# Gate operand sums made one stage earlier, in the space of x, with another order of the gate weights and other accumulator banks

## The chip, the cores and the metric

The kernel runs on one core of a Trainium2 chip. The metric is the device time of one execution in microseconds, lower is better; the median of three runs is 2232.85 us (2231.98 to 2233.49).

## The reference, cut to what matters

One decoder layer on 256 tokens of width 2048, in fp32:

```python
x = layer_norm(ALPHA * x + 0.5 * swiglu(x, ffn1_w_in, ffn1_w_out), ...)
z = x @ mix_w_in                     # conv B | C | h | hgrn q | f | i | g | gate_conv | gate_hgrn
y_conv = short_conv_mixer(b_gate, c_gate, h_conv, conv_w)
y_hgrn = hgrn2_mixer(q_raw, f_raw, i_in, g_raw, lower_bounds, hg_norm_w)
merged = (sigmoid(gate_conv) * (y_conv @ branch_w_conv)      # gate_*: 2048 columns each of z
          + sigmoid(gate_hgrn) * (y_hgrn @ branch_w_hgrn))   # branch weights: 1024 x 2048
x = layer_norm(ALPHA * x + merged @ mix_w_out, ...)
x = layer_norm(ALPHA * x + 0.5 * swiglu(x, ffn2_w_in, ffn2_w_out), ...)
x = layer_norm(ALPHA * x + sigmoid(x @ ple_w_gate) * (p @ ple_w_proj), ...)
```

## The kernel before, in words

All weights (some 430 MB) stream from memory once, in pieces of 512 KB: 256 rows by 512 columns, as a tile of 128 partitions by 1024 numbers. SP issues each load into one of four raw slots (NRAW, tile `raw`, L969). An fp32 product is made of three fast ones: ScalarE casts the raw weight to its high half `wh` (L1029), VectorE subtracts to get the low half `wl` (L1040), and TensorE multiplies high by high, low by high and high by low (L1096, L1097, L1098). The operand x1 (x after the first layer norm, transposed) is kept in such halves too, `xh` and `xl`, made in L288 and L289. The split in L1040 is the last reader of a raw slot, so it lets the next load of that ring start. `wh` and `wl` live in pairs of slots: NMAIN = 6 pairs for all, and EXTRA more in some stages, for the elements that are marked for them (two of eight, in plain units only); a pair comes free when TensorE has used it.

The plan is a list of units: plain ones (`Unit`) and `Quad`s. A Quad computes two column blocks of 512 with seven products for eight, after Strassen's manner, for half of the depth; its weight elements are named in a string (ORDER): `11`, `22`, `21` are loaded pieces, `t1` to `t4` sums of loaded pieces (made by VectorE in L1008 in raw slots of rings of their own, HIGH, where a piece waits until its last sum), each with the step 0 or 1 behind the dot; `a0` to `a3` and `u0` to `u3` are the plain pieces of the other half of the depth, for the first and the second column block. The products of t1, 22, t3 and t2 need sums of x1's four parts, s1 to s4 (tiles `sh`, `sl`).

The stages follow each other: lead1, ffn1, tail1, hgrn, merge, lead2, ffn2, tail2, ple. In the hgrn stage the conv and hgrn parts of z are computed, with the chunked recurrence, and the two mixers' outputs `ya` and `yb` are transposed into halves `gh` and `gl`; its last tiles are b (L768), transposed by TensorE (L278), and `z` (L774). The merge stage has for each of four column blocks c one Quad for the two gates, then two units of four elements each, called conv and hgrn here (`branch_w_conv`, `branch_w_hgrn`; in the texts c.0 to c.3 and h.0 to h.3). Each such element has six products for each of two token tiles t. Then come four units of mix_w_out.

`gate_sums` runs at the head of the merge stage: four additions give x1's parts in whole (L797), `four` (L312) the four combinations, and `halves` (L288, L289) casts and splits them. `settle` and `affine_rows` (L398, L399) apply the first layer norm's scale and shift to the plain x, column block by column block, in the hgrn stage; x itself (two tiles of 128 x 2048) is next read behind the merge stage, at the sum with mix_w_out's result (L876).

Accumulators are eight banks of PSUM; `ptile` gives out the bank whose last handing out is longest ago. `defer` puts small pieces of work some elements later. A scheduler sorts the instructions of each engine by a simulated timeline when the program is built, and each engine then runs its own in that order.

## Time and profile before

| | us |
|---|---|
| median of three runs | 2232.85 |
| the profiled execution | 2234.01 |
| its span, first to last instruction | 2232.3 |
| TensorE busy (98% of the span) | 2192.5 |
| VectorE busy (81%) | 1809.8 |
| ScalarE busy (53%) | 1173.6 |
| GpSimd busy | 10.1 |
| hgrn stage | 720 to 1062 |
| gate quads and branch units | 1062 to 1345 |

The profile is of one execution. Its page gives busy times and the chain of work that ended last; the trace behind it is asked by stretch, engine or line. Matmuls overlap, so a row's duration (0.39 us) is longer than the distance to the next row (0.23 us). Line numbers are those of the kernel before, except in the rows of the changed program below.

### The profile page before, as it was taken

How to read it: one execution, taken by the hardware profiler on the slowest of the kernel's cores; microseconds unless marked ns; L12 is line 12 of the kernel's file. 1: busy time of each engine (PE TensorE's matmuls, PEld its weight loads, DVE VectorE, ACT ScalarE, POOL GpSimd, SP SyncE). 2: the span in 40 equal slices, each digit the busy share in tenths (PEclk: the TensorE clock that was granted, in tenths of full speed). 3: DMA queues.
4: the chain of work that ended last, by engine and by line, in shares of the span. 5: the costliest groups of instructions: out<-in, count | busy, mean ns of one | idle time of the engine just before them, and what ended most of it. 6: DMA issues, size and time to landing. Idle time of an engine off the chain costs nothing.

```text
span 2232.3 us, 27072 instructions
## 1 busy us (share of the span) xinstructions
PE 2192.5 (98%) x10038; PEld 1823.3 (82%) x10038; DVE 1809.8 (81%) x2046; ACT 1173.6 (53%) x1393; POOL 10.1 (0%) x32
## 2 busy tenths in 40 slices
PE   9999999999999999999899999999999999999997
PEld 7988888888877888888687788798888888888886
...
GB/s 255 217 193 205 208 207 192 193 193 208 206 207 105 208 169 172 187 171 156 209 168 185 186 179 217 174 203 193 193 198 198 202 213 200 201 212 178 181 209 153
DMA packets 225848, 429.99 MB, mean 193 GB/s; under 512 B 14252, under 2 KB 22964, under 8 KB 225716
## 3 DMA queue, kind: packets, MB, share of 16 engines
...
q14 instruction: 54, 0.44, 0.1%
...
## 4 chain that ended last, share of the span: by engine, by line
PE 90%; DVE 4%; DMA 2%; ACT 2%; issue 1%; SPq 0%; DVEq 0%; ACTq 0%
PE bank L1097 29%; PE bank L1096 29%; PE bank L1098 29%; DVE wl L1040 2%; PE bank L278 2%; ACT wh L1029 1%; PE bank L634 1%; DVE raw L1008 1%; DMA raw<-in_branch_w_hgrn_dram 1%; DMA raw<-in_ffn_w_in_dram 0%; DMA raw<-in_ffn_w_out_dram 0%; DVE silu L460 0%; DVE x L435 0%; DMA raw<-in_mix_w_in_dram 0%; DMA x<-in_x_dram 0%
## 5 line engine op out<-in xcount | busy, mean ns | idle before, releaser
L1029 ACT CAST wh<-raw 128x1024 fp32r<-128x1024 f32 (+1 forms) x968 | 971.9, 1031 | 802.3 <-PE bank L1098 409.8
L1040 DVE TENSOR_TENSOR wl<-raw,wh 128x1024 fp32r<-128x1024 f32 (+1 forms) x968 | 1137.1, 1201 | 266.7 <-ACT wh L1029 249.4
L1098 PE MATMUL bank<-wh,xl 128*128 128x512 f32 (+1 forms) x1672 | 646.7, 388 | 1.4 <-DVE xl L289 1.4
L1097 PE MATMUL bank<-wl,xh 128*128 128x512 f32 (+1 forms) x1672 | 647.9, 388 | 0.1
L1096 PE MATMUL bank<-wh,xh 128*128 128x512 f32 (+1 forms) x1672 | 639.2, 389 | 2.6 <-ACT xh L288 1.6
L1096 PEld LDWEIGHTS bank<-wh,xh 128*128 128x128 f32 x1672 | 315.5, 189 | 63.5 <-ACT xh L288 2.3
L1098 PEld LDWEIGHTS bank<-wh,xl 128*128 128x128 f32 x1672 | 315.3, 189 | 62.3 <-DVE xl L289 2.3
L1097 PEld LDWEIGHTS bank<-wl,xh 128*128 128x128 f32 x1672 | 315.3, 189 | 59.8 <-DVE wl L1040 0.7
L1096 PE MATMUL bank<-wh,gh 128*128 128x512 f32 x896 | 348.4, 395 | 10.7 <-ACT wh L1029 7.5
L1097 PE MATMUL bank<-wl,gh 128*128 128x512 f32 x896 | 350.8, 393 | 2.6 <-DVE wl L1040 2.2
L1098 PE MATMUL bank<-wh,gl 128*128 128x512 f32 x896 | 349.8, 392 | 0.0
L1008 DVE TENSOR_TENSOR raw<-raw,raw 128x1024 f32<-128x1024 f32 x208 | 245.0, 1181 | 10.6 <-DMA raw<-in_ffn_w_in_dram 7.4
L1096 PEld LDWEIGHTS bank<-wh,gh 128*128 128x128 f32 x896 | 169.2, 189 | 48.4 <-ACT wh L1029 10.4
L1097 PE MATMUL bank<-wl,sh 128*128 128x512 f32 x528 | 206.9, 392 | 0.7 <-DVE wl L1040 0.7
L1098 PE MATMUL bank<-wh,sl 128*128 128x512 f32 x528 | 205.7, 390 | 0.0
L1096 PE MATMUL bank<-wh,sh 128*128 128x512 f32 x528 | 202.4, 390 | 2.5 <-ACT wh L1029 2.5
L1097 PEld LDWEIGHTS bank<-wl,gh 128*128 128x128 f32 x896 | 168.9, 189 | 39.4 <-DVE wl L1040 5.4
L1098 PEld LDWEIGHTS bank<-wh,gl 128*128 128x128 f32 x896 | 168.9, 188 | 34.7
L1096 PEld LDWEIGHTS bank<-wh,sh 128*128 128x128 f32 x528 | 99.1, 188 | 23.8 <-ACT wh L1029 3.2
L1097 PEld LDWEIGHTS bank<-wl,sh 128*128 128x128 f32 x528 | 99.2, 188 | 21.7 <-DVE wl L1040 1.5
L1098 PEld LDWEIGHTS bank<-wh,sl 128*128 128x128 f32 x528 | 99.2, 188 | 20.2
L288 ACT CAST gh<-bank 128x512 fp32r<-128x512 f32 (+2 forms) x54 | 30.6, 569 | 77.5 <-PE bank L278 77.0
...
## 6 DMA issues: line engine op xcount, KB each, us to landing
raw<-in_ffn_w_in_dram SPq DMA_DIRECT2D x288, 512.0 KB, 4.3
...
raw<-in_ffn_w_in_dram SPq DMA_DIRECT2D x64, 256.0 KB, 3.0
...
```

What stands on the lines that cost most here:

```text
L278: state["turned"] = nc.tensor.transpose(tp[:, i * P : (i + 1) * P], src[:, i * P : (i + 1) * P], ident).ins
L288: nc.scalar.copy(hf, src)
L634: nc.tensor.matmul(gp[:, (h * 2 + t) * 64 : (h * 2 + t + 1) * 64], kd[:, h, t * P : (t + 1) * P], qd[:, h, t, :], start=True, stop=True)
L1008: nc.vector.tensor_tensor(out=out, in0=a, in1=b, op=ALU.add)
L1029: nc.scalar.copy(h[:, :n, :w], raw[:, :n, :w])
L1040: state["split"] = nc.vector.tensor_tensor(out=l[:, :n, :w], in0=raw[:, :n, :w], in1=h[:, :n, :w].bitcast(F32), op=ALU.subtract).ins
L1096: nc.tensor.matmul(acc, sh, wh[:, a, :n], start=first, stop=False)
L1097: nc.tensor.matmul(acc, sh, wl[:, a, :n], start=False, stop=False)
L1098: nc.tensor.matmul(acc, sl, wh[:, a, :n], start=False, stop=last)
```

## The change

Five things change together.

1. The sums s1 to s4 are made in the hgrn stage, from the copy of the second v on (`epi_v`, j = 1, first token tile), and not at the head of merge. They use three temporary tiles, and their halves are written into the space of x's two tiles.
2. For this x is stored to device memory, by eight transfers of 256 KB issued from GpSimd, each behind the affine of its column block, and loaded again by eight transfers from GpSimd at the end of the last gate quad.
3. All four quads use one ORDER, "gate", which interleaves a1 to a3 with the other elements; "gate0" is gone.
4. In gate quads a bank counts as used at each write to it (`used`), not only when it is handed out.
5. EXTRA for merge is 2 in place of 0: two more weight pairs, for two of the eight elements of the plain units.

```diff
-EXTRA = {..., "hgrn": 0, "merge": 0, ...}
+EXTRA = {..., "hgrn": 0, "merge": 2, ...}
-        "gate": "a0 a1 11.0 11.1 u0 t1.0 a2 22.0 t3.0 u1 t2.0 21.0 a3 t4.0 u2 t1.1 22.1 t3.1 u3 t2.1 21.1 t4.1",
-        "gate0": "a0 a1 a2 a3 11.0 11.1 u0 t1.0 22.0 t3.0 u1 t2.0 21.0 t4.0 u2 t1.1 22.1 t3.1 u3 t2.1 21.1 t4.1",
+        "gate": "a0 11.0 a1 11.1 a2 t1.0 u0 22.0 t3.0 u1 t2.0 21.0 u2 t4.0 t1.1 u3 22.1 t3.1 a3 t2.1 21.1 t4.1",
+        self.by_end = form == "gate"
     def ptile(role, name):
-        n = min(role_of[role], key=lambda n: used_at[n])
+        bank = banks[min(role_of[role], key=lambda n: used_at[n])]
+        used(bank)
+        return bank
+
+    def used(bank):
+        n = next(n for n in banks if banks[n] is bank)
         used_at[n] = max(used_at.values()) + 1
-        return banks[n]
-    def halves(stat, t, g, src, nb, tag):
+    def halves(stat, t, g, src, nb, tag, into=None):
+    def store_x(c):
+        for t in range(NT):
+            stored[t, c] = dram.tile([P, CC], F32, tag=f"x{t}{c}", name="stored")
+            nc.gpsimd.dma_start(stored[t, c], xt[t][:, c * CC : (c + 1) * CC])
+
+    def load_stored():
+        xt[:] = [res.tile([P, D], F32, tag=f"x{t}", name=f"x{t}") for t in range(NT)]
+        for c in range(4):
+            for t in range(NT):
+                nc.gpsimd.dma_start(xt[t][:, c * CC : (c + 1) * CC], stored[t, c])
+
+    def gate_sums():
+        def both(o, a, b, op):
+            nc.vector.tensor_tensor(out=o, in0=a, in1=b, op=op)
+        def whole(o, t, g):
+            both(o, *(a.rearrange("p a b -> p (a b)").bitcast(F32) for a in x1.parts[t, g]), ALU.add)
+        def made(n, src):
+            i = int(n[1]) - 1
+            into = [w[:, 4 * i : 4 * i + 4, :] for w in room_of_x]
+            halves(x1, n, 0, src, 4, "s", into)
+        room_of_x = [res.tile([P, 16, P], F32R, tag=f"x{t}", name="s") for t in range(NT)]
+        a, b = (rtile([P, CC], tag=f"sum{i}", name="sum") for i in range(2))
+        d = st.tile([P, CC], F32, tag="h", name="sum", bufs=3)
...
+        def s1():
+            whole(a, 1, 0)
+            whole(b, 1, 1)
+            both(b, a, b, ALU.subtract)
+            made("s1", b)
...
+        for i, fn in enumerate((s1, s3, s2, s4)):
+            defer(1 + 4 * i, fn)
+            if not early and stat is x1:          # in affine_rows
+                store_x(c)
         def epi_v(t, acc):
+            if j == 1 and t == 0:
+                gate_sums()
             if c == 3:                            # in gate_units, the last piece of a quad's work
                 share_banks({"a": 4, "t": 4})
+                load_stored()
-        units.append(Quad(x1, wm, cols, CC, after, "gate" if c else "gate0"))
+        units.append(Quad(x1, wm, cols, CC, after, "gate"))
-    units.append(("merge", gate_sums))
+                if u.by_end:                      # in run_quad, at each element
+                    used(ps[bank])
```

In the rows of the changed program below the same work has other line numbers: the products are L1149 to L1151, the cast of a weight L1082, its split L1093, the sum of raw weights L1061, halves L296 and L297, b L834, z L840.

TensorE at the turn from the first gate quad to its branch units. `wh_8880` and `wh_8894` are the first two weights of the hgrn branch (h.0, h.1) before, `wh_8816` the first of the conv branch; `wh_8877`, `wh_8896` and `wh_8910` are h.0, h.1 and h.2 after. Before:

```order
L1096 MATMUL bank0_79<-wh_8880,gh_7132 128x512
L1097 MATMUL bank0_79<-wl_8881,gh_7132 128x512
L1098 MATMUL bank0_79<-wh_8880,gl_7133 128x512
L1096 MATMUL bank0_79<-wh_8894,gh_7132 128x512
L1096 MATMUL bank7_86<-wh_8816,gh_7174 128x512
L1097 MATMUL bank7_86<-wl_8817,gh_7174 128x512
L1098 MATMUL bank7_86<-wh_8816,gl_7175 128x512
L1096 MATMUL bank7_86<-wh_8816,gh_7174 128x512
L1097 MATMUL bank7_86<-wl_8817,gh_7174 128x512
```

After:

```order
L1149 MATMUL bank5_86<-wh_8877,gh_7062 128x512
L1150 MATMUL bank5_86<-wl_8878,gh_7062 128x512
L1151 MATMUL bank5_86<-wh_8877,gl_7063 128x512
L1149 MATMUL bank5_86<-wh_8896,gh_7062 128x512
L1150 MATMUL bank5_86<-wl_8897,gh_7062 128x512
L1151 MATMUL bank5_86<-wh_8896,gl_7063 128x512
L1149 MATMUL bank5_86<-wh_8896,gh_7062 128x512
L1150 MATMUL bank5_86<-wl_8897,gh_7062 128x512
L1151 MATMUL bank5_86<-wh_8896,gl_7063 128x512
L1149 MATMUL bank5_86<-wh_8910,gh_8409 128x512
L1150 MATMUL bank5_86<-wl_8911,gh_8409 128x512
```

Before, TensorE turns to conv behind one product of h.1, and comes back to h.1 at the end of conv's first token tile; after, it goes on through the hgrn branch.

ScalarE in the hgrn stage behind the last affine of x (`r` is the root of the hgrn norm, `b` the tile that the conv part makes). Before:

```order
L671 ACTIVATE junk,ss<-bank_79 128x128 x4
L1029 CAST wh<-raw 128x1024
L367 ACTIVATE r<-w 128x4
L768 COPY b<-bank_86 128x512
L1029 CAST wh<-raw 128x1024 x3
L288 CAST gh<-bank_85 128x512
```

After:

```order
L735 ACTIVATE junk,ss<-bank_81 128x128 x4
L1082 CAST wh<-raw 128x1024
L429 ACTIVATE r<-w 128x4
L296 CAST s<-sum 128x512
L834 COPY b<-bank_88 128x512
L1082 CAST wh<-raw 128x1024 x3
L296 CAST gh<-bank_87 128x512
```

The cast of s1 (`s<-sum`) has come between the root and the copy of b, ahead of three casts of weights.

VectorE at the start of the merge stage; `gl<-z` is the last operand of the hgrn stage. Before:

```order
L774 TENSOR_TENSOR z<-bank_85,cT 128x512
L797 TENSOR_TENSOR xT<-xh,xl 128x512 x4
L289 TENSOR_TENSOR gl<-z,gh 128x512
L312 TENSOR_TENSOR xT<-xT 128x512
L1040 TENSOR_TENSOR wl<-raw_8527,wh 128x1024
L312 TENSOR_TENSOR xT<-xT 128x512
L1040 TENSOR_TENSOR wl<-raw_8529,wh 128x1024
L1008 TENSOR_TENSOR raw_8527<-raw_8527,raw_8531 128x1024
L312 TENSOR_TENSOR xT<-xT 128x512
L1040 TENSOR_TENSOR wl<-raw,wh 128x1024
L289 TENSOR_TENSOR sl<-xT,sh 128x512
L1008 TENSOR_TENSOR raw_8531<-raw_8531,raw_8533 128x1024
```

After:

```order
L840 TENSOR_TENSOR z<-bank_87,cT 128x512
L297 TENSOR_TENSOR gl<-z,gh 128x512
L1093 TENSOR_TENSOR wl<-raw_8548,wh 128x1024
L1093 TENSOR_TENSOR wl<-raw,wh 128x1024
L1061 TENSOR_TENSOR raw_8548<-raw_8548,raw_8552 128x1024
L1093 TENSOR_TENSOR wl<-raw_8550,wh 128x1024
L1093 TENSOR_TENSOR wl<-raw,wh 128x1024
L1061 TENSOR_TENSOR raw_8552<-raw_8552,raw_8554 128x1024
L1093 TENSOR_TENSOR wl<-raw_8548,wh 128x1024
L1093 TENSOR_TENSOR wl<-raw,wh 128x1024
L1093 TENSOR_TENSOR wl<-raw_8554,wh 128x1024
L1061 TENSOR_TENSOR raw_8548<-raw_8548,raw_8554 128x1024
```

The sums, differences and low halves of x1's parts are gone from there, and splits of weights (the a elements among them) stand in their place.

## Rows read from the trace of the kernel before

**Rows 1.** The head of the page: the busy time of TensorE, and the shares of the chain that ended last by engine.

```profile
PE 2192.5 (98%) x10038; PEld 1823.3 (82%) x10038; DVE 1809.8 (81%) x2046; ACT 1173.6 (53%) x1393; POOL 10.1 (0%) x32
PE 90%; DVE 4%; DMA 2%; ACT 2%; issue 1%; SPq 0%; DVEq 0%; ACTq 0%
```

**Rows 2.** Busy time by stretch. Columns: the stretch, its length, then for TensorE, its weight loads, VectorE, ScalarE and GpSimd the busy time and in brackets the number of instructions; behind them the granted TensorE clock, the DMA share and GB/s. The hgrn stage ends at 1062; the merge stage begins there.

```profile
720.00:1062.00 342.00, 342.00 (x1708) 288.89 (x1707) 231.20 (x330) 149.45 (x193) 3.41 (x3) 1.00 0.57 179
1062.00:1072.00 10.00, 9.31 (x42) 7.32 (x40) 9.80 (x13) 5.58 (x7) 0.00 (x0) 1.00 0.48 164
1072.00:1080.00 8.00, 5.76 (x22) 3.79 (x21) 8.00 (x9) 5.43 (x8) 0.00 (x0) 1.00 0.29 84
1080.00:1345.00 265.00, 254.60 (x1116) 208.37 (x1117) 216.10 (x216) 141.09 (x151) 0.00 (x0) 0.98 0.59 188
```

**Rows 3.** What TensorE waited for from 1062 to 1345 us: total, number of waits, longest.

```profile
PE bank L1096 <- ACT wh L1029: 10.6, 7, 5.7
PE bank L1097 <- DVE wl L1040: 2.7, 4, 0.8
```

**Rows 4.** Timeline of TensorE at the turn from the first gate quad to its branch units and behind it: start, duration, engine, line, operation, tiles; in brackets the idle time ahead and what ended it. Left out behind 1111.39 are the ten products up to 1116.08, and behind that the rest of the branch units. The last row is the first product of the second quad.

```profile
1103.45 0.39 PE L1098 MATMUL bank<-wh,xl 128*128 128x512 f32 x1
1109.54 0.80 PE L1096 MATMUL bank<-wh,gh 128*128 128x512 f32 x1 [5.70 <-ACT wh L1029]
...
1111.39 0.63 PE L1098 MATMUL bank<-wh,gl 128*128 128x512 f32 x1
...
1116.08 0.39 PE L1096 MATMUL bank<-wh,gh 128*128 128x512 f32 x1
...
1134.90 0.39 PE L1096 MATMUL bank<-wh,xh 128*128 128x512 f32 x1
```

**Rows 5.** Timeline of TensorE at the same turn of column blocks 1 and 2, and the load ahead of the latter in the chain that ended last (start, duration, what).

```profile
1176.59 0.50 PE L1096 MATMUL bank<-wh,gh 128*128 128x512 f32 x1 [0.72 <-ACT wh L1029]
...
1241.51 0.50 PE L1096 MATMUL bank<-wh,gh 128*128 128x512 f32 x1 [1.05 <-ACT wh L1029]
...
1234.72 5.60 DMA raw<-in_branch_w_hgrn_dram
```

**Rows 6.** Timeline of VectorE at the start of the merge stage: the rows of the operand sums (L797 sums, L289 low halves; the differences, L312, have the size of one low half).

```profile
1062.80 2.49 DVE L797 TENSOR_TENSOR xT<-xh,xl 128x512 f32<-128x512 f32 x4
...
1072.15 0.69 DVE L289 TENSOR_TENSOR sl<-xT,sh 128x512 fp32r<-128x512 f32 x1
...
1080.17 1.90 DVE L289 TENSOR_TENSOR sl<-xT,sh 128x512 fp32r<-128x512 f32 x3
```

**Rows 7.** Timeline of TensorE, VectorE and ScalarE around z: the transposes of b, z, the cast of z, the first cast of a weight behind it; and, of the turn in rows 4, the cast whose product starts at 1109.54.

```profile
1061.56 0.60 PE L278 MATMUL bank<-ident,b 128*128 128x128 f32 x4
...
1062.20 0.69 DVE L774 TENSOR_TENSOR z<-bank,cT 128x512 f32<-128x512 f32 x1 [3.59 <-PE bank L278]
...
1062.92 0.62 ACT L288 CAST gh<-z 128x512 fp32r<-128x512 f32 x1 [5.04 <-DVE z L774]
1063.45 1.04 ACT L1029 CAST wh<-raw 128x1024 fp32r<-128x1024 f32 x1
...
1108.45 1.05 ACT wh L1029
```

**Rows 8.** The chain that ended last behind z: the load of the ring of 12 and the first sum with it.

```profile
1063.97 5.26 DMA raw<-in_mix_w_in_dram
1069.28 1.22 DVE raw L1008
```

**Rows 9.** The chain that ended last ahead of the turn in block 0 (its cast stands in rows 7), and VectorE ahead of it, in the timeline.

```profile
1101.83 1.23 DVE wl L1040
1103.07 5.27 DMA raw<-in_branch_w_hgrn_dram
...
1099.74 0.69 DVE L807 TENSOR_TENSOR sig<-sig,bank 128x512 f32<-128x512 f32 x1 [0.49 <-ACT sig L821]
```

**Rows 10.** Timeline of VectorE in the hgrn stage, two gaps.

```profile
718.63 1.22 DVE L1040 TENSOR_TENSOR wl<-raw,wh 128x1024 fp32r<-128x1024 f32 x1 [3.37 <-ACT wh L1029]
...
933.59 1.23 DVE L599 TENSOR_TENSOR kb<-qT,kT 128x1024 f32<-128x1024 f32 x1 [4.91 <-ACT qT L716]
```

**Rows 11.** Timeline of VectorE (the last affine of the first half of x) and of ScalarE behind it.

```profile
873.32 0.69 DVE L399 TENSOR_TENSOR x<-x,gb 128x512 f32<-128x512 f32 x1 [1.04 <-DMA gb<-in_ln_b_dram]
...
875.02 0.59 ACT L768 COPY b<-bank 128x512 f32<-128x512 f32 x1 [2.59 <-PE bank L1098]
876.38 1.05 ACT L1029 CAST wh<-raw 128x1024 fp32r<-128x1024 f32 x1 [0.77 <-PE bank L1098]
877.75 1.05 ACT L1029 CAST wh<-raw 128x1024 fp32r<-128x1024 f32 x1 [0.31 <-PE bank L1098]
879.11 1.05 ACT L1029 CAST wh<-raw 128x1024 fp32r<-128x1024 f32 x1 [0.31 <-PE bank L1098]
```

**Rows 12.** DMA issues of the page and of the answer for the whole program: median us from issue to landing.

```profile
out_dram<-x SPq DMA_DIRECT2D x8, 256.0 KB, 2.3
x<-in_x_dram SPq DMA_DIRECT2D x8, 256.0 KB, 7.0
```

**Rows 13.** Timeline of GpSimd: its second copy of kb.

```profile
974.00 1.04 POOL L609 COPY kb<-kT 128x1024 f32<-128x1024 f32 x1 [105.01 <-PE bank L604]
```

**Rows 14.** Timeline of VectorE: the first read of x behind the merge stage.

```profile
1347.31 0.69 DVE L876 SCALAR_TENSOR_TENSOR x<-x,bank 128x512 f32<-128x512 f32 x1 [3.13 <-PE bank L1098]
```

49 lines of the change are left out of this document (27 added, 22 removed).

## The prediction

> **What bounds the kernel now.** I read the profile from the outside in. The page says that TensorE is busy for 98% of the span and that 90% of the chain that ended last is its work [rows 1]. The change can therefore only win back time in which TensorE idles, or lose some by new idling. The table by stage shows where there is any [rows 2]: the hgrn stage (720 to 1062 us), into which work is moved, has none, 342.00 of 342.00 us. From 1062 to 1345 us, the merge stage's gate quads and branch units, it lacks 0.69, 2.24 and 10.40 us. The waits of TensorE there say the same by cause: 10.6 us for the high half of a weight (cast on ScalarE) and 2.7 us for the low half (subtracted on VectorE), 13.3 us in all [rows 3]. That is the ceiling of what this change can reach, plus what a low clock costs there. The granted clock is 0.98 of full between 1080 and 1345 us [rows 2]: behind the longest idle time, 5.70 us, the eleven products up to 1116.08 follow each other at 0.43 us, against 0.23 otherwise (1.2 and 2.4 GHz), for 4.7 us from 1111.39 to 1116.08: 11 x 0.20 = 2.2 us [rows 4].
>
> Where the 13.3 us lie matters more than their sum. The single largest loss is the turn from the first gate quad to its branch units: the quad's last product starts at 1103.45, and the next quad's first at 1134.90 [rows 4]. Between them lie 96 products, 96 x 0.227 = 21.8 us (0.227: ScalarE's casts of 876.38, 877.75 and 879.11 each wait for the next six products [rows 11], 1.36 us), in 31.2 us: 9.5 us lost. The same turn waits 0.72 us for a high half in column block 1 and 1.05 in block 2 [rows 5], each with a low half behind it (four such waits make 2.7 us [rows 3]) and a slow product or two, about 2.0 and 2.2 in all; block 3 has none. The start of the stage costs the rest of the 13.3, some 3.8 us.
>
> **The operand sums leave the start of the merge stage.** They are four sums (2.49 us in one row), four differences of 0.69 and four low halves (0.69, and 1.90 for three), some 8 us of VectorE between 1062.8 and 1082 [rows 6], when VectorE is busy 9.80 of 10 and 8.00 of 8 us [rows 2]. One would like to book 3 us of TensorE for that. I book little, because other work comes in. Before, the four a weights are cast and split ahead of the stage, and their 10.9 us of products carry TensorE over the wait for the first loads and sums. In the new order only a0 stands ahead of 11.0, and 11.0's cast stands on ScalarE behind the cast of z. The transposes of b at 1061.56 [rows 7] now stand behind 22 products (a0 and ten of a1), so a0 begins 22 x 0.227 = 5.0 us earlier, at 1056.6, and ends at 1059.3. There they stand in the changed order; b is ready. z follows 0.64 us after the transposes begin, as it does now (1061.56 to 1062.20), its cast 0.72 after that, 11.0's cast 0.53 later, and its product 1.09 later (1108.45 to 1109.54) [rows 4, 7]: 1059.3 + 2.98 = 1062.3. The transposes end at 1059.9: 2.4 us idle which are not there now. VectorE takes over the splits of a1 to a3, 3 x 1.14 = 3.4 us of the 8 freed. The load of 12, behind z in SP's queue, starts some 2.3 us earlier than 1063.97, so that its sum can start at 1067.0 instead of 1069.28 [rows 8]; with sum 1.14 and cast 1.05, t1's first product comes at 1069.3. TensorE has by then 33 of its 180 products, 7.5 us of 40.8 (8 long weights of 2.72, 14 short ones of 1.36), and idles 1.5 us more. If nothing else stops it the quad ends at 1069.3 + 33.3 = 1102.6, against 1103.7 now. VectorE has 18 splits and 7 sums of 1.14 us and 2 or 3 products of 0.7 left at 1068, 30 us, to 1098; it is no longer the bound, but near it, and each wait of its own shows in the end. I take 1103.2: **-0.5 us**, bounds -1.1 and +1.
>
> **The turn to the branch units.** Now TensorE does h.0, begins h.1 and then turns to conv; h.0's load waits for the raw slot that the split of c.0 frees, and that chain is in the trace: split 1.23, load 5.27, cast 1.05 [rows 7, 9], against three short and one long element of TensorE's work. In the changed order hgrn's four weights come first, h.0 to h.3, for blocks 0 to 2. Two of eight branch weights get an extra pair, and in block 0 that is c.3: its cast is ahead of t4.1's in ScalarE's order. With S for the split of a3, which frees c.3's slot, c.3's split ends at S + 5.3 + 1.05 + 1.23 = S + 7.6; t4.1's split, behind it on VectorE, at S + 8.8; h.0's load, started at S + 7.7, gives a cast weight at S + 14.1. TensorE's end of t4.1 hangs on how far S leads the products of a3, behind which 2.72 + 3 x 1.36 = 6.8 us follow. a3's cast needs the pair of u2, six weights earlier, 8.2 us of products ahead of a3; less 1.05 and 1.23 that is a lead of 5.9 at best. VectorE hardly idles now at the end of this quad (0.49 us at 1099.74 [rows 9]), so its splits run close; I take 4. Then t4.1 ends at S + 10.8 and TensorE idles **3.3 us** for h.0, bounds 1.4 (lead 5.9) and 5; h.1 (slot from the split of c.0, one split later) costs 0.8, h.2 0.6, and three loads at 1.2 us spacing share the DMA engines, which I put at 1 to 2 us. Sum 6.2 against 9.5: **-3.3 us**, bounds -6 (lead 5.9, no sharing) and +2 (lead 2.3, the low clock's 2.2 us as now, sharing at twice that). In block 1 the extra pair is c.1's and h.0's slot comes straight from a3's split, so h.0 is in time and only its successors wait: 2.1 against 2.0, **+0.1**. In block 2 c.3 goes ahead again: the chain of 5.60 + 1.05 + 1.23 + 5.60 + 1.05 us [rows 5, 7, 9] against 13 us of products from a3's split at its best lead gives 1.6 us for h.0, then 1.0, 0.8, 1.0 and 0.4 behind it, 4.8 against 2.2: **+2.6**, bounds 0 and +3. Block 3 takes conv first, as now: **0**, bounds 0 and +1.
>
> **The sums arrive in the hgrn stage.** Twelve operations of 0.6 us on VectorE and four casts on ScalarE, where TensorE never waits. The first three fall into VectorE's gap of 3.37 us ahead of 718.63, the others into one of 4.91 us ahead of 933.59 [rows 10]. Cost 0 while those gaps last; without them it would be up to 5 us.
>
> But one of them waits. The sums are put where x lay, and x is first stored. The cast of s1 on ScalarE, placed ahead of a copy at 875.02, where ScalarE is now idle for 2.59 us, waits for the last store of x's first half, which starts after the affine that ends at 874.0; behind it queue the weight casts of 876.38, 877.75 and 879.11, which TensorE waits for five weights later [rows 11]. A cast takes the pair that TensorE let go at 876.35; 5 x 1.36 us later, at 883.2, its product is due, its low half at 883.4, so the cast may start 3.7 us late. No store of this kind is in the trace: the nearest rows, 256 KB each, land in 2.3 us (the output) and 7.0 (x at the start) [rows 12]. From 2.3 that first weight cast is 1.1 us late and nothing is lost; from 7.0 the low half of the first of these weights comes 1 us too late. I take **0**, nearer to the output, the only other store; bounds 0 and +1. POOL gets eight stores and eight loads; its second copy of kb starts at 974.00, but the last store is issued at about 876 [rows 11, 13]. **0**.
>
> **The reload of x** starts after the last use of s2 (about 1304) and is first read at 1347.31 [rows 14]. Eight transfers at the slowest 7.0 us one after another would be 56 us and 13 too late, but sixteen engines have moved several at once everywhere in this trace. **0**, bounds 0 and +3.
>
> **Banks by last write** is what gives the new order of the turn and is counted there.
>
> Sum: -0.5 - 3.3 + 0.1 + 2.6 = -1.1 on the profiled execution's 2234.0 us, 2232.9. That execution is 1.16 us above the median of the runs shown, 2232.85, so on their scale the forecast is 2231.7, rounded **2232**. What a measurement of this kernel can tell from no change is about 0.2%, 4.5 us: **no change**, 0.44.
>
> **Rivals.** *The turns get better throughout* (0.33). The extra pairs let conv casts run ahead; if a3's split leads by its best in every block and the loads don't slow each other, each h weight is nearly in time. For it: block 3 shows a turn without idle time with today's loads of 5.3 us. Against: the raw ring stays at four slots and the six pairs of the quads are unchanged. Half of 9.5 + 2.0 + 2.2 gives -7, 2226; all of it -13.7, 2219; with the start's 3.8 us too, 2215. *The out-of-turn cast costs more than it saves* (0.14). Blocks 0 and 2 put VectorE behind a load that itself waits for a3's split; if TensorE's idle time then drops its clock as the 5.70 us did, each of the two turns costs 2.2 us more and sharing 1.5 in each: -1.1 + 7.4, 2239. It decides as soon as h.0 waits as long as now in block 0. *The store holds ScalarE* (0.09). With landing in over 7 us, each further microsecond is one of TensorE in a stage with none to spare: 12.5 us, if stores from POOL's queue are slower than any here, is -1.1 + 6, 2238.
>
> The Trainium skill has a rule for this ("SBUF — State Buffer", section "SBUF: two separate sides"): descriptors of a transfer issued from GpSimd are written by its cores, and these are locked out of their port while VectorE runs an operation in a two-port mode, so that the transfer seems blocked. By that rule the stores could be late as in the rival above, and the sum would be up to 6 us higher; no row of this trace shows a transfer on POOL's queue, and the work of VectorE at 874 to 882 is mostly of two operands.
>
> **How the numbers follow.** Faster by over 0.2% (under 2228.4): the better turns, 0.33. Slower (over 2237.3): 0.14 + 0.09 = 0.23, both by their mechanisms' prices. Within: 0.44. The bounds of the terms add to -7 and +11 if all went one way. The range leaves out 0.1 below (nearly all turns cured) and 0.1 above: 2223 to 2240.
>
> **What would show it.** Right: TensorE idles about 2.4 us before 11.0's first product and about 3 us before h.0's in block 0; block 2's turn is longer than now; the hgrn stage stays full. Wrong: TensorE rows with an idle time in the hgrn stage behind the cast of s1 (the store), a turn in blocks 0 to 2 without idle time (faster), or the x reload ending after 1347.

## The result, and the profile after

The changed kernel takes 2239.12 us (median; 2235.55 to 2242.20 in 11 runs), the kernel before 2233.97 (2230.19 to 2235.96, 11 runs): ratio 1.0023, 95% interval 1.0013 to 1.0032. It is slower, by some 5 us. The forecast was no change, 2232; the time lies in the range, the direction was missed.

The page of the changed kernel has this for [rows 1]:

```profile
span 2237.4 us, 27109 instructions
PE 2197.3 (98%) x10038; PEld 1823.3 (81%) x10038; DVE 1809.1 (81%) x2046; ACT 1169.6 (52%) x1393; POOL 18.8 (1%) x48
```

The span has grown by 5.1 us and TensorE's busy time by 4.8. The page alone would suggest that TensorE has more to do. It has not: it executes the same 10038 instructions. A product that follows an idle time is counted longer, and at the low clock it is longer. Busy time by stretch, which answers to [rows 2], and the waits of TensorE from 1062 to 1345 us, which answer to [rows 3] (columns as there):

```profile
720.00:1062.00 342.00, 341.15 (x1702) 287.76 (x1700) 234.84 (x338) 150.02 (x196) 7.80 (x11) 1.00 0.56 180
1062.00:1072.00 10.00, 8.32 (x23) 6.28 (x24) 9.19 (x9) 7.73 (x9) 0.00 (x0) 0.66 0.77 254
...
1080.00:1345.00 265.00, 254.69 (x1111) 205.44 (x1110) 209.88 (x211) 137.51 (x150) 4.33 (x8) 0.99 0.60 194
```

```profile
PE bank L1150 <- DVE wl L1093: 5.6, 8, 0.8
PE bank L1149 <- ACT wh L1082: 5.1, 5, 2.4
PE bank L283 <- DVE sig L860: 1.5, 1, 1.5
PE bank L1149 <- DVE sig L860: 0.6, 1, 0.6
```

The waits add to 12.8 us, against 13.3 before, but they are now fifteen short ones, none above 2.38, in place of eleven with one of 5.70. A wait costs more than the idle time in its row, since the product behind it runs 0.1 to 0.4 us longer; so the distance between two fixed products is the better measure. Four such products, called marks from here on, are the first of the second, third and fourth quad and a late one of the first mix_out unit. TensorE's timeline has them like this, the changed kernel first, then the three of before that do not stand in [rows 4]:

```profile
1132.56 0.39 PE L1149 MATMUL bank<-wh,xh 128*128 128x512 f32 x1
...
1199.02 0.39 PE L1149 MATMUL bank<-wh,xh 128*128 128x512 f32 x1
...
1266.12 0.39 PE L1149 MATMUL bank<-wh,xh 128*128 128x512 f32 x1
...
1346.26 0.39 PE L1149 MATMUL bank<-wh,gh 128*128 128x512 f32 x1
```

```profile
1199.50 0.39 PE L1096 MATMUL bank<-wh,xh 128*128 128x512 f32 x1
...
1264.44 0.39 PE L1096 MATMUL bank<-wh,xh 128*128 128x512 f32 x1
...
1341.66 0.39 PE L1096 MATMUL bank<-wh,gh 128*128 128x512 f32 x1
```

| stretch | before | changed | difference | forecast |
|---|---|---|---|---|
| up to the second quad (start, turn of block 0) | 1134.90 | 1132.56 | -2.34 | -3.8 |
| second to third quad (turn of block 1) | 64.60 | 66.46 | +1.86 | +0.1 |
| third to fourth quad (turn of block 2) | 64.94 | 67.10 | +2.16 | +2.6 |
| fourth quad to mix_out (turn of block 3, reload) | 77.22 | 80.14 | +2.92 | 0 |
| sum | | | +4.60 | -1.1 |

The first row carries an offset that is not the change's: at 700 us, where the two programs are still the same, the changed run was already 1.0 us late. Offsets of one or two us of this kind differ from run to run; the other rows are free of them.

**The start.** TensorE's timeline behind the end of the hgrn stage:

```profile
1063.52 0.80 PE L1149 MATMUL bank<-wh,xh 128*128 128x512 f32 x1 [2.38 <-ACT wh L1082]
1064.47 1.22 PE L1149 MATMUL bank<-wh,xh 128*128 128x512 f32 x2 [0.15 <-ACT wh L1082]
1065.49 0.63 PE L1150 MATMUL bank<-wl,xh 128*128 128x512 f32 x1
...
1069.76 0.53 PE L1151 MATMUL bank<-wh,xl 128*128 128x512 f32 x1
```

The idle time of 2.38 us ahead of 11.0's product stands where the prediction put it (2.4). The second one, 1.5 us for t1.0, did not come. Instead eleven products from 1065.49 to 1069.76 follow each other at 0.43 us, half the speed (the granted clock is 0.66 as a mean from 1062 to 1072 us): 11 x 0.20 = 2.2 us.

**The turn of block 0** (ScalarE's cast of h.0, then TensorE, answering to [rows 4]):

```profile
1104.23 1.05 ACT L1082 CAST wh<-raw 128x1024 fp32r<-128x1024 f32 x1 [1.22 <-DMA raw<-in_branch_w_hgrn_dram]
1105.33 0.51 PE L1149 MATMUL bank<-wh,gh 128*128 128x512 f32 x1
1106.59 0.50 PE L1150 MATMUL bank<-wl,gh 128*128 128x512 f32 x1 [0.75 <-DVE wl L1093]
...
1109.32 0.50 PE L1149 MATMUL bank<-wh,gh 128*128 128x512 f32 x1 [1.29 <-ACT wh L1082]
1110.58 0.50 PE L1150 MATMUL bank<-wl,gh 128*128 128x512 f32 x1 [0.76 <-DVE wl L1093]
```

h.0 is in time now, its low half and h.1 are not. The steps that the prediction priced can be read from the trace. The split of a3 ends at 1092.74 (its S), and c.3's load starts there and lands 4.90 us later; c.3's split ends at 1100.00, S + 7.3. h.0's load then takes 4.10 us, and its cast ends at 1105.28, S + 12.5, where the prediction had 14.1. The quad's last product ends at S + 12.5 as well, where it had 10.8: the split of a3 leads by 5.7 us, not by 4. So h.0's wait of 3.3 us did not come. What came is 2.8 us for its successors and, behind them, seven products at some 0.43 us from 1111.25 on (granted clock 0.50 from 1111.0 to 1114.4), some 1.5 us. From h.0's first product, about 0.1 us behind the quad's end, to the next quad this turn takes 1132.56 - 1105.33 = 27.2 us; before it took 31.2.

**The turn of block 1** (answering to [rows 5]): the four waits of TensorE, then ScalarE's and VectorE's rows ahead of them.

```profile
1174.33 0.50 PE L1150 MATMUL bank<-wl,gh 128*128 128x512 f32 x1 [0.48 <-DVE wl L1093]
...
1176.10 0.51 PE L1149 MATMUL bank<-wh,gh 128*128 128x512 f32 x1 [0.34 <-ACT wh L1082]
...
1177.36 0.50 PE L1150 MATMUL bank<-wl,gh 128*128 128x512 f32 x1 [0.75 <-DVE wl L1093]
...
1181.43 0.50 PE L1150 MATMUL bank<-wl,gh 128*128 128x512 f32 x1 [0.67 <-DVE wl L1093]
```

```profile
1169.21 2.94 ACT L1082 CAST wh<-raw 128x1024 fp32r<-128x1024 f32 x3
1170.30 3.24 SPq L1022 DMA_DIRECT2D raw<-in_branch_w_hgrn_dram  x3
1170.79 3.49 DVE L1093 TENSOR_TENSOR wl<-raw,wh 128x1024 fp32r<-128x1024 f32 x3
...
1175.00 1.05 ACT L1082 CAST wh<-raw 128x1024 fp32r<-128x1024 f32 x1 [2.85 <-DMA raw<-in_branch_w_hgrn_dram]
```

The third of the splits at 1170.79 ends at 1174.28, just ahead of the first low half that TensorE waits for. As splits free raw slots, SP issues three hgrn loads, at 1170.30, 1172.03 and 1173.17; the next cast begins at 1175.00, when the first of them has landed, 1.5 us behind the quad's end (1173.46). TensorE, which in this order wants all four hgrn weights ahead of conv's, meets one after another a little late.

**Block 2** is much like block 1: h.0 is in time here too (c.3's load took 4.6 us and h.0's 3.7, where the prediction had 5.60 for each), and four waits of 0.61, 0.95, 0.76 and 0.76 us follow.

**Block 3**: GpSimd's issue of the reload, ScalarE, VectorE and TensorE, and a load in the chain that ended last.

```profile
1304.55 4.33 POOL L372 DMA_DIRECT2D x<-stored  x8 [328.31 <-PE bank L1151]
...
1313.04 1.05 ACT L1082 CAST wh<-raw 128x1024 fp32r<-128x1024 f32 x1 [5.12 <-DMA raw<-in_branch_w_hgrn_dram]
1314.12 1.23 DVE L1093 TENSOR_TENSOR wl<-raw,wh 128x1024 fp32r<-128x1024 f32 x1 [4.34 <-ACT wh L1082]
1315.27 0.69 DVE L860 TENSOR_TENSOR sig<-sig 128x512 f32<-128x512 f32 x1
...
1316.60 1.36 PE L283 MATMUL bank<-ident,m 128*128 128x128 f32 x8 [1.45 <-DVE sig L860]
1319.68 0.50 PE L1149 MATMUL bank<-wh,gh 128*128 128x512 f32 x1 [0.57 <-DVE sig L860]
...
1306.01 10.62 DMA raw<-in_branch_w_hgrn_dram
```

The load of 10.62 us, beside the eight transfers of the reload, is h.3's; h.2's, issued at 1304.88, took 8.07 (median of all loads of this kind here: 5.2). TensorE did not wait for these weights themselves. It waited for gate sums on VectorE, which stood in VectorE's order behind the splits of the late weights: h.2's split is the row with 4.34 us idle ahead of it, and the wait of 1.45 us comes from the sums behind it; h.3's split, at 1317.81, stands ahead of the sum that ended the wait of 0.57.

**The store** did what the prediction bounded. ScalarE's cast of s1, and the landing times of the two new transfers:

```profile
877.95 0.62 ACT L296 CAST s<-sum 128x512 fp32r<-128x512 f32 x1 [4.40 <-DMA stored<-x]
```

```profile
stored<-x POOLq DMA_DIRECT2D x8, 256.0 KB, 4.6
x<-stored POOLq DMA_DIRECT2D x8, 256.0 KB, 8.4
```

The store that this cast waited for landed in 2.4 us. VectorE's low half of s1, which the prediction did not ask about, waited 1.35 us for another that took 5.3. The weight casts behind the cast of s1 [rows 11] began at 878.95, 2.6 us later than 876.38 (the offset of 1.0 included), less than the 3.7 that were allowed, and TensorE waited for nothing between 720 and 1049 us.

### The profile page after: what moved, and what is told of

It is laid out like the page before. It is cut to its first block, busy times and chain, and to the rows that moved or that the text cites. A ratio compares the mean times of both kernels' runs of the same rounds, so it can differ in the third digit from the quotient of the medians.

```text
span 2237.4 us, 27109 instructions
## 1 busy us (share of the span) xinstructions
PE 2197.3 (98%) x10038; PEld 1823.3 (81%) x10038; DVE 1809.1 (81%) x2046; ACT 1169.6 (52%) x1393; POOL 18.8 (1%) x48
## 4 chain that ended last, share of the span: by engine, by line
PE 90%; DVE 4%; DMA 3%; ACT 2%; issue 1%; DVEq 0%; SPq 0%; ACTq 0%
PE bank L1150 29%; PE bank L1149 29%; PE bank L1151 29%; DVE wl L1093 2%; PE bank L283 2%; ACT wh L1082 1%; DMA raw<-in_branch_w_hgrn_dram 1%; PE bank L698 1%; DMA raw<-in_ffn_w_in_dram 0%; DMA raw<-in_branch_w_conv_dram 0%; DMA raw<-in_mix_w_in_dram 0%; DVE raw L1061 0%; DVE x L499 0%; DVE x L500 0%; DMA raw<-in_ffn_w_out_dram 0%
## 5 line engine op out<-in xcount | busy, mean ns | idle before, releaser
L1082 ACT CAST wh<-raw 128x1024 fp32r<-128x1024 f32 (+1 forms) x968 | 969.3, 1031 | 824.3 <-PE bank L1151 405.9
L1093 DVE TENSOR_TENSOR wl<-raw,wh 128x1024 fp32r<-128x1024 f32 (+1 forms) x968 | 1135.1, 1199 | 272.2 <-ACT wh L1082 258.2
L1151 PE MATMUL bank<-wh,xl 128*128 128x512 f32 (+1 forms) x1672 | 647.4, 388 | 1.7 <-DVE xl L297 1.7
L1149 PE MATMUL bank<-wh,xh 128*128 128x512 f32 (+1 forms) x1672 | 639.8, 390 | 4.5 <-ACT wh L1082 2.5
L1149 PEld LDWEIGHTS bank<-wh,xh 128*128 128x128 f32 x1672 | 315.9, 189 | 65.8 <-ACT wh L1082 3.3
L1151 PEld LDWEIGHTS bank<-wh,xl 128*128 128x128 f32 x1672 | 315.9, 189 | 63.0 <-DVE xl L297 2.3
L1149 PE MATMUL bank<-wh,gh 128*128 128x512 f32 x896 | 348.1, 394 | 6.1 <-ACT wh L1082 4.0
L1151 PE MATMUL bank<-wh,gl 128*128 128x512 f32 x896 | 349.0, 391 | 0.0
L1061 DVE TENSOR_TENSOR raw<-raw,raw 128x1024 f32<-128x1024 f32 x208 | 245.1, 1179 | 15.7 <-DMA raw<-in_ffn_w_in_dram 7.3
L1149 PEld LDWEIGHTS bank<-wh,gh 128*128 128x128 f32 x896 | 168.6, 188 | 45.5 <-ACT wh L1082 8.2
L1151 PEld LDWEIGHTS bank<-wh,gl 128*128 128x128 f32 x896 | 168.5, 188 | 34.5
L1150 PE MATMUL bank<-wl,sh 128*128 128x512 f32 x464 | 181.6, 391 | 0.0
L1151 PE MATMUL bank<-wh,sl 128*128 128x512 f32 x464 | 180.5, 389 | 0.0
L1149 PE MATMUL bank<-wh,sh 128*128 128x512 f32 x464 | 177.1, 389 | 0.0
L1149 PEld LDWEIGHTS bank<-wh,sh 128*128 128x128 f32 x464 | 87.1, 188 | 18.3
L1151 PEld LDWEIGHTS bank<-wh,sl 128*128 128x128 f32 x464 | 87.1, 188 | 17.9
L1150 PEld LDWEIGHTS bank<-wl,sh 128*128 128x128 f32 x464 | 87.1, 188 | 17.8
L296 ACT CAST gh<-bank 128x512 fp32r<-128x512 f32 (+2 forms) x54 | 30.7, 570 | 76.1 <-PE bank L283 75.5
```

What stands on the lines that cost most here:

```text
L296: nc.scalar.copy(hf, src)
L1061: nc.vector.tensor_tensor(out=out, in0=a, in1=b, op=ALU.add)
L1082: nc.scalar.copy(h[:, :n, :w], raw[:, :n, :w])
L1093: state["split"] = nc.vector.tensor_tensor(out=l[:, :n, :w], in0=raw[:, :n, :w], in1=h[:, :n, :w].bitcast(F32), op=ALU.subtract).ins
L1149: nc.tensor.matmul(acc, sh, wh[:, a, :n], start=first, stop=False)
L1150: nc.tensor.matmul(acc, sh, wl[:, a, :n], start=False, stop=False)
```

## The experiments

The expectations number their theories as they came up. At the end the question was whether the time went to the extra pairs, the new order, the banks or the reload, and then why the turns idle in every version. Ahead of all, the marks of every run (distances as in the table above; "to quad 1" is the mark of the second quad, an absolute time that carries the run's offset; each ratio is to the kernel before as it was run beside the version, with medians of 2233.57 to 2234.71 us):

| run | to quad 1 | block 1 | block 2 | block 3 | median, us | ratio to before (95%) |
|---|---|---|---|---|---|---|
| before | 1134.90 | 64.60 | 64.94 | 77.22 | 2233.97 | |
| changed | 1132.56 | 66.46 | 67.10 | 80.14 | 2239.12 | 1.0023 (1.0013 to 1.0032) |
| e1_reload_later | 1130.34 | 67.97 | 68.04 | 77.36 | 2236.10 | 1.0014 (1.0004 to 1.0023) |
| e2_no_extra | 1129.99 | 65.96 | 65.56 | 77.38 | 2230.36 | 0.9985 (0.9975 to 0.9995) |
| e3_old_banks | 1134.70 | 71.75 | 73.43 | 83.51 | 2253.42 | 1.0091 (1.0076 to 1.0106) |
| e5_both | 1135.06 | 71.65 | 72.74 | 78.05 | 2249.46 | 1.0071 (1.0056 to 1.0086) |
| e6_no_extra_gate0 | 1128.81 | 66.30 | 66.76 | 77.38 | 2231.13 | 0.9983 (0.9974 to 0.9993) |
| e7_order_alone | 1139.06 | 68.88 | 68.52 | 77.20 | 2244.90 | 1.0045 (1.0030 to 1.0059) |
| e8_sums_alone | 1130.61 | 64.89 | 65.15 | 77.34 | 2230.04 | 0.9979 (0.9970 to 0.9989) |
| e10_banks_alone | 1137.37 | 66.18 | 65.42 | 77.25 | 2237.03 | 1.0009 (1.0000 to 1.0018) |
| g0_before_swap | 1135.55 | 64.49 | 66.56 | 77.23 | 2234.21 | 1.0000 (0.9991 to 1.0010) |
| g1_sums_swap | 1129.31 | 64.70 | 64.74 | 77.34 | 2229.01 | 0.9979 (0.9969 to 0.9988) |
| g2_no_extra_swap | 1130.15 | 65.68 | 65.68 | 77.38 | 2230.81 | 0.9987 (0.9978 to 0.9996) |
| g3_changed_swap | 1129.33 | 66.47 | 68.75 | 79.26 | 2237.86 | 1.0019 (1.0010 to 1.0028) |
| h0_before_keep | 1130.78 | 62.56 | 62.56 | 77.23 | 2224.52 | 0.9953 (0.9938 to 0.9968) |
| h1_sums_keep | 1123.41 | 62.66 | 62.67 | 77.33 | 2217.10 | 0.9921 (0.9905 to 0.9938) |
| h2_noextra_keep | 1124.42 | 63.49 | 62.69 | 77.38 | 2220.69 | 0.9942 (0.9927 to 0.9957) |
| h3_after_keep | 1132.21 | 69.41 | 67.82 | 81.78 | 2239.19 | 1.0024 (1.0014 to 1.0033) |

### The reload and the extra pairs

**e1_reload_later**: the changed kernel, the reload cut in four pieces, each held back on GpSimd behind work of block 3 and after.

```
-            for t in range(NT):
-                nc.gpsimd.dma_start(xt[t][:, c * CC : (c + 1) * CC], stored[t, c])
+        for t in range(NT):
+            nc.gpsimd.tensor_copy(xt[t][:, c * CC : c * CC + 1], behind[:, :1])
+            nc.gpsimd.dma_start(xt[t][:, c * CC : (c + 1) * CC], stored[t, c])
```

> The changed kernel, with the reload of x held back until the hgrn branch of block 3 has its sums, in four pieces. Theory 1 (the reload slows the loads of the hgrn branch's weights in block 3, of which one took 10.62 us where 5.2 is usual, and splits and products queue behind it): TensorE's waits of 1.45 and 0.57 us in block 3 go, the stretch from the end of the fourth quad to the first late mix_out product is 36 to 37 us in place of 39.2, and the time falls by 2 to 3 us, to about 2236.5. Rival (the new order of VectorE's products in block 3 makes the waits, and the reload is hidden): nothing falls, 2239.

Measured 2236.10, 3.0 below the changed kernel. Block 3 falls from 80.14 to 77.36, the length of before, and the transfers of the reload land in 5.4 us. So the 2.9 us of block 3 need the reload beside the last hgrn loads. Blocks 1 and 2 of this run are 1.5 and 0.9 longer than the changed kernel's. In both its clock fell: it is 0.50 from 1176.8 to 1180.1 us and from 1245.1 to 1248.4, products at 0.43 us in place of 0.23, some 1.6 us a time, where the changed kernel's stays at 1.00.

**e2_no_extra**: the changed kernel without the extra pairs.

```
-EXTRA = {..., "merge": 2, ...}
+EXTRA = {..., "merge": 0, ...}
```

> The changed kernel without the two extra weight pairs in merge. The hgrn branch still comes first at the turns of blocks 0 to 2, but only its first two weights; then conv, then the other two. Theory 1 (loss at the turn comes from hgrn weights that are wanted before they are loaded): with two wanted early the turns last about 24 us each in place of 27.2, 25.6 and 26.2, and the time falls by 5 to 8 us, to about 2232. Rival (the extra pairs are what shortens the turn of block 0 by 4 us): that turn goes back to 31 us and the time rises by 2 to 4, to about 2242.

Measured 2230.36: taking the pairs away is worth 8.8 us, more than the whole loss, and turns it into a gain. Block 3 is 77.38 with the reload where the change put it, landing nearly as slowly as there (7.8 us). Its last two hgrn loads are as late too, 7.91 and 10.76 us. VectorE has them in another order: the last gate sums, then the splits of these two weights.

```profile
1308.08 1.88 DVE L860 TENSOR_TENSOR sig<-sig,bank 128x512 f32<-128x512 f32 x3
...
1314.22 2.60 DVE L1093 TENSOR_TENSOR wl<-raw,wh 128x1024 fp32r<-128x1024 f32 x2 [1.06 <-ACT wh L1082]
```

So the reload costs only together with the extra pairs; in the rows of block 3 above it is the split of a late hgrn weight, ahead of the gate sums, that passes its delay on to TensorE.

### Order, banks and sums apart

**e8_sums_alone**: the kernel before with the sums in the hgrn stage, the store and the reload, nothing else; written from the changed kernel:

```
-EXTRA = {..., "merge": 2, ...}
+EXTRA = {..., "merge": 0, ...}
-        "gate": "a0 11.0 a1 11.1 a2 t1.0 u0 22.0 ...",
+        "gate": "a0 a1 11.0 11.1 u0 t1.0 a2 22.0 ...",
+        "gate0": "a0 a1 a2 a3 11.0 11.1 u0 t1.0 22.0 ...",
-        self.by_end = form == "gate"
+        self.by_end = False
```

> The kernel before with the operand sums made in the hgrn stage in the space of x, with the stores and the reload, and nothing else of the change. The turns stand as before. Theory 2: VectorE is relieved by 8 us where it is full, TensorE's waits between 1071 and 1089 us fall from 3.8 to 1 us or less, the reload costs 0 to 1 us in block 3, and the time falls by 2 to 3 us, to about 2231. Rival (the reload slows block 3 as in the changed kernel, 2.8 us): no change, 2233.5.

Measured 2230.04, 0.9979: some 4.7 us gained. From 1049 to 1100 us TensorE is busy for 50.67 of 51 us (47.13 before, 48.47 changed); all waits at the start are gone. The turns idle as before (6.24 us at h.0 in block 0). The reload costs nothing here either: h.3's load beside it took 12.60 us, more than in the changed kernel, its split stands behind the gate sums, and block 3 is 77.34.

e2 differs from this run in the new order and the new banks, and takes the same time (2230.36). So of the five changes the earlier sums, with the store and reload that make room for them, gain some 4 to 5 us, the order and the banks on top of them nothing, and the pairs lose 8.8.

**e7_order_alone**: the kernel before with the new ORDER for all four quads.

```
-        "gate": "a0 a1 11.0 11.1 u0 t1.0 a2 ...",
-        "gate0": "a0 a1 a2 a3 11.0 ...",
+        "gate": "a0 11.0 a1 11.1 a2 t1.0 u0 ...",
```

> The kernel before with the new order of the gate weights alone (one order for all four quads). Conv comes first at every turn. Theory 2 (with banks by their handing out conv gets a bank whose gate sum the last products of the quad still hold up; the new order puts these at the very end): TensorE waits 5 to 8 us for a gate product at each turn, as with the changed kernel with old banks, and the time is 2248 to 2256. Rival (those waits need the extra pairs): no such waits, turns under 24 us, time about 2228.

Measured 2244.90, 10 or 11 us above before, less than the 2248 to 2256 that were forecast. TensorE takes conv first at each turn and waits for the bank, 8.41, 4.43 and 4.09 us in blocks 0 to 2. In block 0 its last reader is a gate sum:

```profile
1114.50 0.77 PE L1095 MATMUL bank<-wh,gh 128*128 128x512 f32 x1 [8.41 <-DVE sig L806]
```

**e10_banks_alone**: the kernel before with banks by last write (`self.by_end = form.startswith("gate")`, and `used(ps[bank])` at each element).

> The kernel before with banks by last write in the gate quads alone. Two hgrn weights come first at the turns. Theory 2 (h.0's load waits for the split of c.0 whatever the banks): TensorE still idles about 5 us for h.0 in block 0 and 1 us in blocks 1 and 2; the time is 2232 to 2236. Rival (the banks alone shorten the turns): the turn of block 0 is 27 us or less in place of 31.2, and the time falls to about 2229.

Measured 2237.03, 1.0009 (1.0000 to 1.0018): no gain; h.0 in block 0 still idles 6.59 us.

**e3_old_banks**: the changed kernel with banks as before, `self.by_end = False`.

> The changed kernel with banks given out by their last handing out, as before; all else as changed. Conv comes first at every turn. Theory 1: the hgrn weights are then loaded while conv is multiplied, the turns of blocks 0 to 2 last 22 to 23 us each (21.8 is without idle time) in place of 27.2, 25.6 and 26.2, and the time falls by 10 to 13 us, to about 2227. Rival (conv first must wait for banks that VectorE's gate products still read, which is what banks by last write avoid): TensorE waits for those products at each turn, the turns stay at 25 us or more, and the time is within 3 us of 2239.

Measured 2253.42, the slowest of all. Theory 1 fell; the rival's mechanism held, but it had put the time within 3 us of 2239, and it is 14 above. In block 1 ScalarE, VectorE and TensorE had

```profile
1177.79 1.04 ACT L1082 CAST wh<-raw 128x1024 fp32r<-128x1024 f32 x1 [3.60 <-DMA raw<-in_branch_w_hgrn_dram]
...
1178.86 1.23 DVE L1093 TENSOR_TENSOR wl<-raw,wh 128x1024 fp32r<-128x1024 f32 x1 [2.70 <-ACT wh L1082]
...
1182.34 0.68 DVE L860 TENSOR_TENSOR sig<-sig,bank 128x512 f32<-128x512 f32 x1
...
1183.16 0.77 PE L1149 MATMUL bank<-wh,gh 128*128 128x512 f32 x1 [7.39 <-ACT sig L866]
```

Read from the bottom: TensorE waits for a bank that the gate stage still reads. Its row names ScalarE's sigmoid (L866), which reads no bank; of the work that reads one, the gate sum at 1182.34 ends last, at 1183.02. This sum stands in VectorE's order behind a split; the split waits for a cast, and the cast for an hgrn load.

**e5_both**: e3 and e1 together (`by_end = False`, the reload held back).

> The changed kernel with the old rule of banks and the later reload of x together. Theory 1: both gains, 12 to 16 us under the changed kernel, about 2225, so clearly faster than the kernel before too. Rival of either: only one of the two gains, 2227 to 2236.

Measured 2249.46, outside both forecasts, since the old banks cost time instead of winning it: block 3 falls from 83.51 to 78.05, so the reload is the cause there in this version too; the bank waits of blocks 0 to 2 stay.

**e6_no_extra_gate0**: e2 with the old order of the first quad alone (`"gate" if c else "gate0"`).

> The changed kernel without the extra pairs, and the first quad in its old order (a0 to a3 ahead), the other three in the new one. Theory 2 (the new order costs at the start of merge, 2.38 us idle and some 2 us of low clock, and gains at the turn of block 0, because the late a3 frees a raw slot early enough for h.0): the start gains 3 to 4 us, the turn of block 0 goes back from 24 to 29 us or more, and the time is about 2232, against 2230.4 without this edit. Rival (the turn is short by the banks alone): the turn stays at 24 us and the time falls to about 2227.

Measured 2231.13, no different from e2. The waits at the start go, and 5.64 us ahead of h.0 in block 0 come back: with a0 to a3 first, conv's weights and h.0 have to wait for slots again. What the new order wins at this turn it pays at the start.

An experiment with the extra pairs alone on the kernel before was not run: as the kernel is laid out, the pairs have their place only because x is stored away meanwhile.

### Why the turns idle

**g0 to g3**: hgrn's unit ahead of conv's in the plan of blocks 0 to 2, so that its weights are loaded first; on before (g0), on e8 (g1), on e2 (g2) and on the changed kernel (g3). The addition of the two parts moves along, to the end of the unit that is now second (left out here).

```
-        units.append(Unit(ya, branch_w_conv[0], 0, 8, c * CC, CC, epi_c))
-        units.append(Unit(yb, branch_w_hgrn[0], 0, 8, c * CC, CC, epi_h))
+        pair = [Unit(ya, branch_w_conv[0], ...), Unit(yb, branch_w_hgrn[0], ...)]
+        units.extend(pair if c == 3 else pair[::-1])
```

> The kernel before, with the hgrn unit ahead of the conv unit in blocks 0 to 2, so that its weights are loaded first, in the order in which TensorE has been seen to want them. Theory 3 (the turns idle because the weights wanted first stand behind four others in the load order): the turns of blocks 0 to 2 shrink from 31.2, 23.6 and 24.0 to about 22.5 us each, and the time falls by about 11 us, to 2223. Rival (whatever comes first at the turn is late, since the raw slots come free too late): the waits stay with the other unit's weights, turns as now, 2231 to 2235.

> The operand sums alone moved (2230.0 measured), plus hgrn ahead of conv in blocks 0 to 2. Theory 3: both gains, some 4 and 11 us under the kernel before, about 2219. Rival: the turns keep their waits, 2228 or more.

> The changed kernel without the extra pairs (2230.4 measured), plus hgrn ahead of conv in blocks 0 to 2. Its turns are 23.9 us each. Theory 3: they fall to about 22, 6 us in all, to 2224; the start keeps its 2.38 us of waiting and the low clock. Rival: turns as they are, 2229 or more.

> The changed kernel whole, with hgrn ahead of conv in blocks 0 to 2. Theory 3 (the extra pairs cost time only because they let TensorE want all four hgrn weights first): turns of about 22 us in place of 27.2, 25.6 and 26.2, the wait for the reload in block 3 stays, and the time falls by about 12 us to 2227. Rival (the extra pairs cost time by themselves, by casting two weights out of turn): turns of 25 us or more, 2235 to 2239.

Theory 3 fell: each is within 1.3 us of its kernel without the swap (g0 2234.21, g1 2229.01, g2 2230.81, g3 2237.86), and the waits stay (g0: 5.25 us at block 0). The rows of g0 show why. TensorE's first branch product, and ScalarE's cast ahead of it:

```profile
1109.90 0.79 PE L1100 MATMUL bank<-wh,gh 128*128 128x512 f32 x1 [5.25 <-ACT wh L1033]
```

```profile
1108.80 1.04 ACT L1033 CAST wh<-raw 128x1024 fp32r<-128x1024 f32 x1 [3.55 <-DMA raw<-in_branch_w_conv_dram]
```

Now it is a conv weight that comes late: TensorE takes the unit that is second in the plan first, whichever it is. That left the banks as the reason (theory 4): the unit that is first in the plan gets the banks that come free last.

**h0 to h3**: conv and hgrn exchange their pairs of banks in blocks 0 to 2; on before (h0), e8 (h1), e2 (h2) and the changed kernel (h3).

```
+        units[-1].keeps = c < 3          # behind the conv unit
+                    if keeps and t == 0:
+                        kept[:] = [ptile("a", "acc") for _ in range(NT)]
-                    accs[t] = ptile("a", "acc")
+                    accs[t] = kept.pop(0) if kept and not keeps else ptile("a", "acc")
```

> The kernel before with the exchange of banks alone at the turns of blocks 0 to 2. Theory 4: the waits for wh of 6 us at block 0 and 2 at blocks 1 and 2 go, the waits at the start of the gate stage stay, and the time is 2224 to 2230 us. Rival 5: conv waits for a bank, and the time is 2235 to 2250.

> The kernel before with the operand sums moved to the hgrn stage alone, and at the turns of blocks 0 to 2 the conv unit and the hgrn unit exchange their pairs of banks, so that the unit whose weights are loaded first also gets the bank that is free first. Theory 4 (the bank decides which unit TensorE takes first, and its weights are the ones loaded second): conv's first product starts the turn with its weights there, the waits for wh (4.87 to 6.24 us at block 0, about 2 at blocks 1 and 2) go, and the time is 2220 to 2226 us. Rival 5 (the bank that conv gets is then still being read by the gate stage): conv's or hgrn's first product waits 2 to 8 us for a gate sum as with the old banks, and the time is 2232 to 2245.

> The changed kernel without the extra pairs, with the same exchange of banks at the turns of blocks 0 to 2. Theory 4: the turns fall from about 24 us each to 22 or 23, and the time is 2226 to 2229 us (2230.4 without the exchange). Rival 5: a wait for a gate sum of 2 to 8 us at each turn, 2236 to 2250.

> The changed kernel with the exchange of banks at the turns of blocks 0 to 2. Theory 4: with all eight weights prepared as pairs the first product is conv's, whose pairs are ready, and hgrn's pairs have the time of conv's products; the excess of the turns of 27.2, 25.6 and 26.2 us over 24 goes, the 2.8 us of block 3 stay, and the time is 2230 to 2234 us. Rival 5: the time is that of the changed kernel or above, 2237 to 2255.

Theory 4 held without the extra pairs, and in h1 and h2 beyond its forecast: 2224.52, 2217.10 and 2220.69. Blocks 1 and 2 fall by 2 to 3 us against the same kernel without the exchange, to 62.6 to 63.5, and the mark of the second quad comes 4 to 7 us earlier (offsets included). h1 beats both kernels; it is the best version of the study, 0.9921 of before. TensorE's waits in h1 from 1049 to 1337 us, and its turn of block 0:

```profile
PE bank L1151 <- DVE sig L861: 2.6, 1, 2.6
```

```profile
1097.21 0.39 PE L1151 MATMUL bank<-wh,gh 128*128 128x512 f32 x1
...
1106.54 0.47 PE L1151 MATMUL bank<-wh,gh 128*128 128x512 f32 x1 [2.60 <-DVE sig L861]
1106.85 0.40 PE L1152 MATMUL bank<-wl,gh 128*128 128x512 f32 x1
1107.08 0.40 PE L1153 MATMUL bank<-wh,gl 128*128 128x512 f32 x1
```

One wait of 2.6 us is left of 13.3, for the bank that hgrn has got in exchange, 24 products of conv behind the turn; conv's first product (1097.21) starts without any.

With the extra pairs it fell: h3 takes 2239.19, the same as without the exchange, as its rival said. Its block 1, VectorE and TensorE:

```profile
1177.62 1.23 DVE L1094 TENSOR_TENSOR wl<-raw,wh 128x1024 fp32r<-128x1024 f32 x1 [3.34 <-ACT wh L1083]
1178.76 0.68 DVE L860 TENSOR_TENSOR sig<-sig,bank 128x512 f32<-128x512 f32 x1
...
1183.56 0.74 PE L1150 MATMUL bank<-wh,gh 128*128 128x512 f32 x1 [4.85 <-DVE sig L860]
```

The same pattern as in e3 and in block 3: VectorE stands at a split whose weight has not landed, and the gate sums that would let conv's second bank go are queued behind it. h2, which differs from h3 in the extra pairs alone, has no such wait over 0.5 us.

## Why the prediction was wrong

Without the offset the marks moved by +3.6 us (4.6 - 1.0), where -1.1 was forecast. Of these 4.7 us, 2.9 are block 3 and 1.8 block 1; the other terms came out near their size, but not all for the reason given. Of the signs that it named, the idle time of some 2.4 us ahead of 11.0's first product came, block 2's turn grew and the hgrn stage stayed full; the 3 us ahead of h.0 in block 0 did not come.

- **The ceiling** was read rightly: all that the change could win were 13.3 us of waits and some slow products, and h1 shows that nearly all of it can be had.
- **The start, -0.5**: the quad with its start measured +0.4 (47.1 to 47.5 us from a0's first product to its end). The first idle time came as worked out (2.38 us), the second, 1.5 us, did not come, and the 2.2 us of half-speed products behind the first were not in the sum. The sums alone are worth some 4.7 us (e8); with the new order the start has this idle time and these slow products instead.
- **Block 0, -3.3**: -4.0 (31.2 to 27.2). The size came out by luck. The wait for h.0, 3.3 of the 6.2 us that were expected there, did not come: a3's split led by 5.7 us, not 4, and h.0's load took 4.10 us, not 5.27. The successors and the low clock (some 1.5 us, not in the sum) cost more than expected instead.
- **Block 1, +0.1**: +1.9. This step failed. "h.0 is in time" held, but its successors were put at 2.1 us, and the turn lost 3.8 (25.6 against 21.8 without idle time): 2.24 in four waits, the rest in the longer products behind them. Before, it lost 1.8.
- **Block 2, +2.6**: +2.2. This size was luck too. The prediction expected 1.6 us for h.0 behind c.3's load; h.0 was in time, and the loss is that of block 1, in the successors. The chain through c.3, which was to set blocks 0 and 2 apart from block 1, never set the time.
- **The store, 0**: right. By the rule of the Trainium skill ("SBUF — State Buffer", section "SBUF: two separate sides") transfers issued from GpSimd can be held up while VectorE runs an operation in a two-port mode. The stores landed in a median of 4.6 us, while VectorE ran its splits and affines; nothing here shows a transfer blocked, and no run shows whether any of that work was in such a mode.
- **Block 3 and the reload, 0**: +2.9, the step that failed most. I asked whether the reload would be in time for its own reader, and it was. What it does to the other loads, 8.07 and 10.62 us in place of 5.2, I covered only by the upper bound. e1 shows that holding the reload back takes the 2.9 us away; e2 and e8 show that the same reload, with loads as late, costs nothing without the extra pairs.
- **What lay behind both failures** was the extra pairs. The prediction gave them no term of their own: they were casts that run ahead in its first rival, and a weight cast out of turn in blocks 0 and 2. They cost 8.8 us (e2). With them TensorE takes all four hgrn weights ahead of conv's at the turns of blocks 0 to 2, as they land, where without them it turns to conv's ready ones after two; and in block 3 splits of weights that have not landed stand ahead of gate sums on VectorE.
- **The rival** "the out-of-turn cast costs more than it saves" has the time, 2239, and the right part of the change, but not its mechanism: it was to decide where h.0 waits as long as before in block 0, and h.0 did not wait there. "Banks by last write" and the order, which I counted at the turn, can't be had one by one: the order alone costs 10 us, the banks alone win nothing, and with the old banks the change loses 14 us more. Together they keep the time of the moved sums alone (e2 and e8), and no more.

What stays open: how the 8.8 us of the extra pairs divide. By the marks of e2 some 2.6 lie ahead of the second quad (0.1 of it offset), 0.5 and 1.5 in blocks 1 and 2, 2.8 in block 3, and 1.4 behind it, where I have no cause. And why the scheduler's order with more pairs puts the splits where it does was not tried by itself.
